# Linear ReLU attention on one core: first K and V issued inside the tile part, thirteen TensorE turns in one block, loads in runs of two, engines held to the last store

## Chip, core and metric

The kernel runs on one core of a Trainium2 chip. The metric is the device time of one execution in microseconds (us). For the kernel before, three runs gave a median of 124.86 us (124.73 to 124.92). A separate profiled execution took 124.66 us; its trace spans 123.4 us from the first to the last instruction of the program.

## What is computed

Q, K, V and the output are 8 x 12 x 512 x 64 in f32: 96 heads, 12.58 MB each. Cut to what matters:

```python
Q_feat = np.maximum(0, Q); K_feat = np.maximum(0, K)
KV = np.einsum('bhkd,bhkv->bhdv', K_feat, V)
K_sum = np.sum(K_feat, axis=2)
numerator = np.einsum('bhqd,bhdv->bhqv', Q_feat, KV)
denominator = np.einsum('bhqd,bhd->bhq', Q_feat, K_sum)
return numerator / (denominator[..., None] + 1e-10)
```

## The kernel before

**Tiling.** The 96 heads go in 12 octets of 8 heads. In an octet each of the 128 partitions holds 32 rows of one head, so Q, K, V and the output of an octet are each one transfer of 1.05 MB on the side of the DRAM. K and V of octet 0 come as f32 on the queues of SP and ACT (L94, L95) into two of the output buffers. All other loads are issued by POOL (L96, L109), which turns them into bf16 on the way, so they show as 512 KB.

**Buffers.** Loads go round a ring of six octets (`RING`, `slot`). Octet o is loaded when octet o-6 has been used: POOL waits on `PR1`, `VC` or `STG`. Results go round nine output buffers (`NOUT`). Each DMA has a semaphore of its own that counts 16 parts; `arrived` makes an engine wait for all 16 once.

**POOL's queue** is written out by hand: for each run of `RUNS` it issues K, V and Q of the run's octets in one DMA each, and ahead of a run the stores that are more than `RING + HEAD` octets behind. Before, each run has one octet and `HEAD` is 4, so store 0 stands ahead of the loads of octet 10, store 1 ahead of those of octet 11, and the rest behind. SP issues the last two stores, 10 and 11. The semaphore ahead of every store is `NRM1`.

**TensorE (PE)** runs `turn(i)` in a loop. In turn i, for octet i-1: 16 transposes of Q (L158; waits `STG`, and `DEN` after eight); 64 matmuls that accumulate K^T V with the row of K sums (L167; wait `VC`, `PR0`, `PR1`); 16 transposes that turn back the *previous* octet's numerators (L148, `back`; wait `OT`); 16 matmuls for the denominators (L176; wait `KVD`); 8 for the numerators (L184; wait `NRM0`, `NRM1`). After the twelve turns, `back` for octet 11 stands by itself behind the loop. An alignment to 256 instructions stands ahead of the loop.

**VectorE (DVE)**, in order for each octet o: wait `CK0`; `prep(o+1, 0)` (K features L237, needs K; V rows L241, needs V); `stage(o+1)` (copy of Q, L247, needs Q); `norm(o-1)` (two multiplies of 1.2 us, L259, write the output buffer; wait for `back`); `denominators(o)` (L265 to L273); `prep(o+1, 1)`. The engine works in order, so what waits for a load holds up everything behind it.

**ScalarE (ACT)**, for each octet: two ReLU evictions of Q^T (L214), four casts of K^T V (L219), V rows of the next octet (L208, needs V), two copies of the numerators (L228), which release `OT`.

**Head and tail.** The framework's part (`tc.close`, L15) ends with two barriers of all engines; then the kernel's own instructions begin, with 18 memsets and four operations on the identity on DVE. At the end SP waits for each store's semaphore in turn (L318) and clears the semaphores; the other engines run out of their programs when their work is done.

Of the kernel before, what the change touches and what calls it, by code (L numbers as in the profile page):

```python
# [5 lines left out]
def kernel(  # L6
# [4 lines left out]
    out: bass.AP,  # L11
):
    nc = tc.nc

    tc.close()  # L15
    tc.compile()

    B, H, S, D = Q.shape
    assert D == 64
    P = 128  # L20
    D1, D4 = D + 1, D + 4
    R = S * 4 // P
    RQ = 2 * R
    U = RQ // 2
    NO = B * H // 8
    assert NO * 8 == B * H and R == 16
    RING = 6
    NOUT = 9
    RUNS = (1,) * 11
    HEAD = 4  # L30

    fp32 = mybir.dt.float32
    bf16 = mybir.dt.bfloat16
    Act = mybir.ActivationFunctionType
    Alu = mybir.AluOpType
    PE, PL, VE, AC, SP = nc.tensor, nc.gpsimd, nc.vector, nc.scalar, nc.sync
# [25 lines left out]
    k8, v8 = o_sb[0], o_sb[1]  # L62
# [4 lines left out]
    vo = [sb(f"vo{i}", [P, R, 2, D4], bf16) for i in range(2)]  # L67
# [13 lines left out]
    ID, STG, PR0, PR1, DEN, NRM0, NRM1, DV = sems(  # L81
        "id", "stg", "pr0", "pr1", "den", "nrm0", "nrm1", "dv")
    VC, KVD, OT = sems("vc", "kvd", "ot")
    CQ0, CQ1, CK0, CK1, CB0, CB1, CD, CO0, CO1 = sems(
        "cq0", "cq1", "ck0", "ck1", "cb0", "cb1", "cd", "co0", "co1")
    landed = {}
    stored = sems(*[f"st{o}" for o in range(NO)])

    def land(name):
        landed[name], = sems(name)  # L90
        return landed[name]


    SP.dma_start(out=k8.rearrange("p r d -> p (r d)"), in_=Kr[0]).then_inc(land("k0"), 16)  # L94
    AC.dma_start(out=v8.rearrange("p r d -> p (r d)"), in_=Vr[0]).then_inc(land("v0"), 16)  # L95
    PL.dma_start(out=q_all[:, RING], in_=Qr[0], single_packet=True).then_inc(land("q0"), 16)  # L96
    run_of = {0: 0}

# [24 lines left out]
    o, done = 1, 0  # L123
# [6 lines left out]
    assert o == NO  # L130
    for i in range(done, NO - 2):
        store(PL, i)
    for i in range(NO - 2, NO):
        store(SP, i)

# [2 lines left out]
    def arrived(eng, c, o):  # L138
        s = landed[f"{c}{run_of[o]}"]
        if (eng.engine, s.num) not in seen:  # L140
            seen.add((eng.engine, s.num))
            eng.wait_ge(s, 16)

    def back(j):
        for v in range(8):
            t = PE.transpose(ps_o[j][:, P * v:P * v + P], ot[:, 8 * j + v].rearrange("p h c -> p (h c)"), ident32)  # L148
        t.then_inc((CB0, CB1)[j], 1)
# [35 lines left out]
                              start=True, stop=True, skip_group_check=True)  # L185
            t.then_inc((CO0, CO1)[j], 1)

    PE.wait_ge(ID, 4)
    with nc.Fori(1, NO + 1, engines=bass.OrderedEngineSet([PE.engine]), head_slot={PE.engine: 0}) as i:
        turn(i)  # L190
    PE.wait_ge(OT, NO + 1)
    back(0)
    back(1)


    def v_rows(o, g):
        rows = slice(R * g, R * g + R)
        return v_all[:, slot(o), rows] if o > 0 else v8[:, rows]
# [5 lines left out]
    def v_scalar(o):  # L204
        arrived(AC, "v", o)
        if o == 0:
            AC.wait_ge(ID, 4)
        AC.activation(vo[0][:, :, 1, 2:D + 2], v_rows(o, 0), Act.Copy, scale=mask_v[:, 1:2]).then_inc(VC, 1)  # L208

    v_scalar(0)  # L210
    for o in range(NO):
# [17 lines left out]
                        ps_o[j].rearrange("p (h u c) -> p u h c", h=4, u=U))  # L229
        t.then_inc(OT, 1)  # L230


    def prep(o, g):

        arrived(VE, "k", o)
        for s in range(2):
            VE.tensor_scalar(kf[g][:, :, s, :], k_rows(o, g), scalar1=0.0,  # L237
                             scalar2=mask_k[:, s:s + 1], op0=Alu.max, op1=Alu.mult)
        arrived(VE, "v", o)
        for t in range(1 + g):  # L240
            x = VE.tensor_scalar(vo[g][:, :, t, 2:D + 2], v_rows(o, g), scalar1=mask_v[:, t:t + 1],  # L241
                                 scalar2=None, op0=Alu.mult)
        x.then_inc((PR0, PR1)[g], 1)
# [5 lines left out]
    def norm(o):  # L249
        dst = o_sb[(o + 2) % NOUT]  # L250
        if o >= NOUT:
            VE.wait_ge(stored[o - NOUT], 16)
        VE.wait_ge(DV, 2 * o + 2 + DV0)
        if o == NOUT - 1:
            VE.wait_ge(VC, 1)
        for j in range(2):
            rs = slice(R * j, R * j + R)
            VE.wait_ge((CB0, CB1)[j], o + 2)
            VE.tensor_tensor(dst[:, rs], ps_o[j].rearrange("p (r d) -> p r d", d=D),  # L259
                             rec[o % 2][:, rs].unsqueeze(2).to_broadcast([P, R, D]),  # L260
                             op=Alu.mult).then_inc((NRM0, NRM1)[j], 1)
# [10 lines left out]
        VE.wait_ge(DV, 2 * o + 1 + DV0)  # L272
        VE.reciprocal(rec[o % 2], den).then_inc(DV, 1)  # L273

    for t in range(2):
        VE.memset(mask_v[:, t:t + 1], 0.0)
    VE.memset(kvd.rearrange("p h d -> p (h d)").bitcast(fp32), 0.0)
    VE.memset(ot.rearrange("p u h c -> p (u h c)"), 0.0).then_inc(OT, 1)
    ones = [vo[g][:, :, :, 1:D4 - 1][:, :, :, 0:D + 2:D1] for g in range(2)]
    VE.memset(ones[0], 0.0)  # L280
    VE.memset(ones[1], 0.0).then_inc(DV, 1)
    VE.wait_ge(DV, 1)
    for t in range(2):
        for half in range(2):
            b = 64 * half + 32 * t
            VE.memset(mask_v[b:b + 32, t:t + 1], 1.0)
            for g in range(2):
                VE.memset(ones[g][b:b + 32, :, t], 1.0)
    VE.wait_ge(ID, 2)
    VE.tensor_copy(ident32, ident).then_inc(ID, 1)  # L290
    VE.wait_ge(ID, 3)
    for c in range(2):
        VE.tensor_reduce(out=mask_h[:, :, c], in_=ident32.rearrange("p (h b) -> p h b", h=8),
                         op=Alu.add, axis=mybir.AxisListType.X)
    VE.tensor_reduce(out=mask_k, in_=ident32.rearrange("p (t s b) -> p s t b", t=4, s=2),
                     op=Alu.add, axis=mybir.AxisListType.XY).then_inc(ID, 1)
    DV0 = 1
    VE.wait_ge(ID, 4)
    for s in (DEN, NRM0, NRM1):
        VE.sem_inc(s, 1)  # L300
    prep(0, 0)
    prep(0, 1)
    stage(0)
    for o in range(NO):
        if o + 1 < NO:
            VE.wait_ge(CK0, o + 1)
            prep(o + 1, 0)
            stage(o + 1)
        if o > 0:
            norm(o - 1)  # L310
        denominators(o)
        if o + 1 < NO:
# [37 lines left out]
```

## Time and profile before

| what | value |
|---|---|
| median of three runs | 124.86 us |
| profiled execution | 124.66 us |
| its span | 123.4 us |
| PE, DVE, ACT, POOL busy | 71%, 72%, 64%, 22% of the span |
| HBM read and written | 37.75 MB and 12.58 MB: 408 GB/s over the span |
| DMA engines from 3 us to 120 us | busy 90% or more in each slice |
| first K and V issued | 1.40 us |
| last multiply on DVE (`norm(11)`, second half) | 115.41 to 116.64 us |
| last load (Q of octet 11) taken up by DVE | 98.52 us |

How to read it: the DMA line gives the busy share of the 16 DMA engines in 40 slices of 3.08 us. The line of GB/s counts what is written: a load that turns f32 to bf16 counts half, so 213 in the load stage and 425 in the store stage are the same 425 GB/s on the DRAM side. One transfer of an octet (1.05 MB there) takes 2.46 us at that rate, and there are 48 of them. In the timeline a row has the start, the busy time, the engine, the line, the operation and, in brackets, the idle time before it and what ended it. The page also lists two queues of kind "instruction": the engines' own fetches of their programs, which run on the same 16 DMA engines.

### The profile page before, as it was taken

The page shows a single profiled execution, that of the slowest core. Times are in us where ns is not written, and L with a number is a line of the kernel's source. Part 1 is how long each engine was busy: PE and PEld are TensorE (multiplying, and loading weights), DVE is VectorE, ACT ScalarE, POOL GpSimd, SP SyncE. Part 2 cuts the span into 40 slices and gives each one's busy share as a digit, 9 for nine tenths or more (in the row PEclk, how much of TensorE's full clock was granted, in tenths as well). Part 3 has the DMA queues.
Part 4 walks back from the last instruction along what each step waited for, and adds up shares of the span by engine and source line. Part 5 has one row for each costly group of instructions (what it writes and reads, how often), then busy time and mean ns, then how long its engine had stood idle before and what let it go on. Part 6 is the DMA issues. An engine that isn't in the chain of part 4 may idle for free.

```text
span 123.4 us, 3380 instructions
## 1 busy us (share of the span) xinstructions
PE 87.4 (71%) x1456; PEld 75.9 (62%) x1456; DVE 89.3 (72%) x178; ACT 79.4 (64%) x109; POOL 27.5 (22%) x50
## 2 busy tenths in 40 slices
PE   0000099998998979799897998979449939977400
PEld 0000099986886868688686877958429928947200
DVE  3737906599989899998989989897395497091600
ACT  0043063999988888898888889888539649542000
POOL 3999500050240804309101001010010001000000
PEclk9999999999999999999999999999985995996775
DMA  3999999999999999999999999999999999999994
GB/s 43 369 344 217 213 213 213 213 215 213 214 213 213 213 215 213 214 214 217 214 213 214 213 214 221 371 217 214 375 222 214 343 425 428 425 422 433 420 425 170
DMA packets 6918, 32.57 MB, mean 264 GB/s; under 512 B 768, under 2 KB 768, under 8 KB 5120
## 3 DMA queue, kind: packets, MB, share of 16 engines
q0 software_dynamic: 6336, 28.31, 92.2%
q1 hardware_dynamic: 432, 3.15, 6.6%
q10 hardware_dynamic: 144, 1.05, 2.2%
q8 instruction: 2, 0.03, 0.1%
q14 instruction: 4, 0.03, 0.1%
HBM read 37.75 MB, written 12.58 MB: 408 GB/s over the span
## 4 chain that ended last, share of the span: by engine, by line
DMA 34%; issue 27%; POOL 18%; PE 8%; DVE 5%; ACT 1%; POOLq 0%; DVEq 0%
DMA q_all<-in_Q_dram 34%; POOL k_all L109 6%; POOL q_all L109 5%; POOL v_all L109 5%; DVE o_sb L259 5%; PE ps_o L148 4%; PE ps_kv L167 2%; PE ps_q L158 1%; PE ps_o L184 1%; POOL out_dram L117 1%; ACT ot L228 1%; POOL q_all L96 1%; POOL ident L121 0%; POOL ident L119 0%; POOLq L107 0%
## 5 line engine op out<-in xcount | busy, mean ns | idle before, releaser
L259 DVE TENSOR_TENSOR o_sb<-ps_o,rec 128x1024 f32<-128x1024 f32 x24 | 28.3, 1219 | 7.0 <-PE ps_o L148 6.7
L228 ACT COPY ot<-ps_o 128x1024 f32<-128x1024 f32 x24 | 24.2, 1013 | 10.3 <-PE ps_o L184 9.2
L167 PE MATMUL ps_kv<-vo,kf 64*128 64x132 bf16 x768 | 28.6, 230 | 0.7
L148 PE MATMUL ps_o<-ident,ot 128*128 128x128 f32 x208 | 27.1, 286 | 1.1 <-ACT ot L228 1.1
L167 PEld LDWEIGHTS ps_kv<-vo,kf 64*128 64x128 bf16 x768 | 24.8, 100 | 3.8 <-DVE vo L241 2.3
L214 ACT ACTIVATE qt_sb<-ps_q 128x1024 bf16<-128x1024 bf16 x24 | 23.4, 1030 | 5.1 <-PE ps_q L158 5.1
L158 PE MATMUL ps_q<-ident,q_sb 128*128 128x128 bf16 x192 | 15.3, 243 | 15.4 <-DVE q_sb L247 15.4
L148 PEld LDWEIGHTS ps_o<-ident,ot 128*128 128x128 f32 x208 | 23.8, 146 | 2.7 <-ACT ot L228 1.4
L158 PEld LDWEIGHTS ps_q<-ident,q_sb 128*128 128x128 bf16 x192 | 13.2, 110 | 16.7 <-DVE q_sb L247 15.4
L219 ACT CAST kvd<-ps_kv 64x260 bf16<-64x260 f32 x48 | 18.0, 375 | 7.8 <-PE ps_kv L167 7.4
L184 PE MATMUL ps_o<-qt_sb,kvd 128*128 128x256 bf16 x96 | 15.0, 282 | 10.8 <-DVE o_sb L259 9.8
L237 DVE TENSOR_SCALAR kf<-k_all,mask_k 128x1024 bf16<-128x1024 bf16 x44 | 18.3, 459 | 5.6 <-PE ps_kv L167 5.4
L184 PEld LDWEIGHTS ps_o<-qt_sb,kvd 128*128 128x128 bf16 x96 | 7.7, 100 | 15.6 <-DVE o_sb L259 15.0
L241 DVE TENSOR_SCALAR vo<-v_all,mask_v 128x1024 bf16<-128x1024 bf16 x33 | 15.0, 483 | 0.9 <-DMA v_all<-in_V_dram 0.9
L109 POOL DMA_DIRECT2D k_all<-in_K_dram x11 | 8.4, 763 | 32.1 <-DVE vo L241 32.0
L117 POOL DMA_DIRECT2D out_dram<-o_sb x10 | 5.3, 533 | 40.7 <-DVE o_sb L259 40.7
L208 ACT ACTIVATE vo<-v_all,mask_v 128x1024 bf16<-128x1024 bf16 x11 | 12.7, 1155 | 0.3
L247 DVE COPY q_sb<-q_all 128x2048 bf16<-128x2048 bf16 x12 | 8.3, 694 | 5.7 <-DMA q_all<-in_Q_dram 5.7
L109 POOL DMA_DIRECT2D q_all<-in_Q_dram x11 | 8.9, 811 | 0.0
L109 POOL DMA_DIRECT2D v_all<-in_V_dram x11 | 7.6, 687 | 0.0
L176 PE MATMUL ps_q<-kvd,qt_sb 128*128 128x16 bf16 x192 | 6.9, 180 | 0.0
L176 PEld LDWEIGHTS ps_q<-kvd,qt_sb 128*128 128x128 bf16 x192 | 6.7, 96 | 0.2
(24 smaller groups left out, 27.8 us busy)
## 6 DMA issues: line engine op xcount, KB each, us to landing
out_dram<-o_sb POOLq DMA_DIRECT2D x10, 1024.0 KB, 39.8
q_all<-in_Q_dram POOLq DMA_DIRECT2D x12, 512.0 KB, 36.7
k_all<-in_K_dram POOLq DMA_DIRECT2D x11, 512.0 KB, 33.1
v_all<-in_V_dram POOLq DMA_DIRECT2D x11, 512.0 KB, 34.8
out_dram<-o_sb SPq DMA_DIRECT2D x2, 1024.0 KB, 8.4
o_sb<-in_K_dram SPq DMA_DIRECT2D x1, 1024.0 KB, 8.5
o_sb<-in_V_dram ACTq DMA_DIRECT2D x1, 1024.0 KB, 8.8
```

Source lines behind the costliest of these rows:

```text
L109: PL.dma_start(out=t[:, to:to + n], in_=X[o:o + n].rearrange("n p f -> p n f"), single_packet=True).then_inc(land(f"{c}{o}"), 16)
L148: t = PE.transpose(ps_o[j][:, P * v:P * v + P], ot[:, 8 * j + v].rearrange("p h c -> p (h c)"), ident32)
L158: t = PE.transpose(dst[:, u], q_sb[:, j * (U // 2) + u], ident)
L167: t = PE.matmul(ps_kv[:, half, 0:2 * (D + 2)].rearrange("p (t d) -> p t d", t=2), kf[g][rows, r].rearrange("p s d -> p (s d)"), vo[g][rows ...
L176: t = PE.matmul(ps_den[:, u], qt_sb[:, u], kvd[:, :, 0:2 * D1:2 * D1 - 1], start=True, stop=True, skip_group_check=True)
L184: t = PE.matmul(ps[:, h], kvd[:, 4 * j + h, 1:2 * D + 1], q[:, :, 4 * j + h, :], start=True, stop=True, skip_group_check=True)
L214: AC.activation(qt_sb[:, j * (U // 2):(j + 1) * (U // 2)], ps_q[j].bitcast(bf16).rearrange("p (u f) -> p u f", u=U // 2), Act.Relu)
L219: t = AC.copy(kvd[64 * c:64 * c + 64, s::2, c * D1:c * D1 + D1].rearrange("p (g t) d -> p g t d", t=2), ps_kv[64 * s:64 * s + 64, :, 0:2 * ...
L228: t = AC.copy(ot[:, :, 4 * j:4 * j + 4], ps_o[j].rearrange("p (h u c) -> p u h c", h=4, u=U))
L237: VE.tensor_scalar(kf[g][:, :, s, :], k_rows(o, g), scalar1=0.0, scalar2=mask_k[:, s:s + 1], op0=Alu.max, op1=Alu.mult)
L241: x = VE.tensor_scalar(vo[g][:, :, t, 2:D + 2], v_rows(o, g), scalar1=mask_v[:, t:t + 1], scalar2=None, op0=Alu.mult)
L259: VE.tensor_tensor(dst[:, rs], ps_o[j].rearrange("p (r d) -> p r d", d=D), rec[o % 2][:, rs].unsqueeze(2).to_broadcast([P, R, D]), op=Alu. ...
```

## The change

- K and V of octet 0 are issued inside the framework's part, in a critical section of SP and ACT, ahead of its closing barriers; PE's alignment moves ahead of that section.
- PE runs 13 turns instead of 12 and a separate `back`. The thirteenth works on old data up to `back`, which serves octet 11, and its last two parts are not used. Other engines raise `STG`, `PR0`, `PR1`, `VC`, `KVD` once more for it.
- DVE's setup shrinks from 18 memsets and four operations to two memsets and five operations; in `norm` the wait for `DV` goes, and `prep` gets one.
- `RUNS` becomes (1, 1, 2, 2, 2, 1, 1, 1): octets 3 and 4, 5 and 6, 7 and 8 are loaded in pairs, with one semaphore for each pair's K, V and Q. `HEAD` is 5, `NOUT` 11.
- At the end PE, ACT, DVE and POOL wait (`hold`) until all stores have landed, and then release SP. Nine stores share one semaphore, the last two another.

```diff
-    tc.close()
-    tc.compile()
...
-    NOUT = 9
-    RUNS = (1,) * 11
-    HEAD = 4
+    NOUT = 11
+    RUNS = (1, 1, 2, 2, 2, 1, 1, 1)
+    HEAD = 5
...
-    stored = sems(*[f"st{o}" for o in range(NO)])
+    ALL, LAST, FIN = sems("all", "last", "fin")
+    stored = [sems(f"st{o}")[0] if o + NOUT < NO else ALL if o < NO - 2 else LAST for o in range(NO)]
...
-    SP.dma_start(out=k8.rearrange("p r d -> p (r d)"), in_=Kr[0]).then_inc(land("k0"), 16)
-    AC.dma_start(out=v8.rearrange("p r d -> p (r d)"), in_=Vr[0]).then_inc(land("v0"), 16)
+    def hold(eng):
+        eng.wait_ge(ALL, 16 * (NOUT - 2))
+        eng.wait_ge(LAST, 32)
+        eng.sem_inc(FIN, 1)
+    PE.addr_align(256, offset=0, max_nops=0)
+    with tc.tile_critical(no_gpsimd_drain=True):
+        SP.dma_start(out=k8.rearrange("p r d -> p (r d)"), in_=Kr[0]).then_inc(land("k0"), 16)
+        AC.dma_start(out=v8.rearrange("p r d -> p (r d)"), in_=Vr[0]).then_inc(land("v0"), 16)
+    tc.close()
+    tc.compile()
...
-    PE.wait_ge(ID, 4)
-    with nc.Fori(1, NO + 1, engines=bass.OrderedEngineSet([PE.engine]), head_slot={PE.engine: 0}) as i:
+    with PE.Fori(1, NO + 2) as i:
         turn(i)
-    PE.wait_ge(OT, NO + 1)
-    back(0)
-    back(1)
+    hold(PE)
...
+    AC.wait_ge(KVD, NO)
+    AC.wait_ge(VC, NO)
+    AC.sem_inc(KVD, 1)
+    AC.sem_inc(VC, 1)
+    hold(AC)
...
+            if t and o:
+                VE.wait_ge(DV, 2 * o + DV0)
...
-        VE.wait_ge(DV, 2 * o + 2 + DV0)
+        if o == NO - 1:
+            VE.wait_ge(DV, 2 * o + 2 + DV0)
...
+    for s in (STG, PR0, PR1):
+        VE.wait_ge(s, NO)
+        VE.sem_inc(s, 1)
     norm(NO - 1)
-    for s in stored:
-        SP.wait_ge(s, 16)
+    hold(VE)
+    SP.wait_ge(CO1, NO + 1)
+    SP.wait_ge(FIN, 4)
```

More of the change, by code (lines that the diff above doesn't have):

```diff
@@ L66 @@
     kf = [sb(f"kf{i}", [P, R, 2, D], bf16) for i in range(2)]
-    vo = [sb(f"vo{i}", [P, R, 2, D4], bf16) for i in range(2)]
+    vo_all = sb("vo", [P, 2, R, 2, D4], bf16)
+    vo = [vo_all[:, i] for i in range(2)]
     kvd = sb("kvd", [P, 8, 2 * D1], bf16)
@@ L132 @@
         store(PL, i)
+    hold(PL)
     for i in range(NO - 2, NO):
@@ L206, in v_scalar @@
         if o == 0:
-            AC.wait_ge(ID, 4)
+            AC.wait_ge(ID, 5)
         AC.activation(vo[0][:, :, 1, 2:D + 2], v_rows(o, 0), Act.Copy, scale=mask_v[:, 1:2]).then_inc(VC, 1)
@@ L273, in denominators @@
         VE.reciprocal(rec[o % 2], den).then_inc(DV, 1)
-    for t in range(2):
-        VE.memset(mask_v[:, t:t + 1], 0.0)
-    VE.memset(kvd.rearrange("p h d -> p (h d)").bitcast(fp32), 0.0)
+    VE.memset(kvd.rearrange("p h d -> p (h d)").bitcast(fp32), 0.0).then_inc(DEN, 1)
     VE.memset(ot.rearrange("p u h c -> p (u h c)"), 0.0).then_inc(OT, 1)
[L279 to L288, printed above, removed]
     VE.wait_ge(ID, 2)
@@ L291 @@
     VE.wait_ge(ID, 3)
-    for c in range(2):
-        VE.tensor_reduce(out=mask_h[:, :, c], in_=ident32.rearrange("p (h b) -> p h b", h=8),
-                         op=Alu.add, axis=mybir.AxisListType.X)
+    VE.tensor_reduce(out=mask_v, in_=ident32.rearrange("p (a t b) -> p t a b", a=2, t=2),
+                     op=Alu.add, axis=mybir.AxisListType.XY).then_inc(ID, 1)
     VE.tensor_reduce(out=mask_k, in_=ident32.rearrange("p (t s b) -> p s t b", t=4, s=2),
-                     op=Alu.add, axis=mybir.AxisListType.XY).then_inc(ID, 1)
-    DV0 = 1
+                     op=Alu.add, axis=mybir.AxisListType.XY).then_inc(NRM0, 1)
+    VE.tensor_reduce(out=mask_h, in_=ident32.rearrange("p (h b) -> p h b", h=8).unsqueeze(2).to_broadcast([P, 8, 2, 16]),
+                     op=Alu.add, axis=mybir.AxisListType.X).then_inc(NRM1, 1)
     VE.wait_ge(ID, 4)
-    for s in (DEN, NRM0, NRM1):
-        VE.sem_inc(s, 1)
+    VE.tensor_copy(vo_all.rearrange("p g r t d -> p (g r) t d")[:, :, :, 1:D4 - 1][:, :, :, 0:D + 2:D1],
+                   mask_v.unsqueeze(1).unsqueeze(3).to_broadcast([P, 2 * R, 2, 2])).then_inc(ID, 1)
+    DV0 = 0
+    VE.wait_ge(ID, 5)
     prep(0, 0)
```

## The prediction

> **What bounds the kernel now.** I read the slices of the page first, then the DMA queues, the tail in small windows, and DVE's timeline. From the page:
>
> ```profile
> DMA  3999999999999999999999999999999999999994
> ...
> q8 instruction: 2, 0.03, 0.1%
> q14 instruction: 4, 0.03, 0.1%
> ```
>
> No engine bounds it: the transfers fill the span from the second slice to the last but one. 48 transfers of 2.46 us are 118.0 us of the 123.4. What can be won lies at the head, the tail, and in how evenly the 16 DMA engines finish. The last two rows are the engines' fetches of their own programs; they look like nothing. But the windows of the tail:
>
> ```profile
> 120.00:121.00 1.00, 0.00 (x0) 0.00 (x0) 0.00 (x0) 0.00 (x0) 0.00 (x0) 0.50 0.99 418
> 121.00:121.50 0.50, 0.00 (x0) 0.00 (x0) 0.00 (x0) 0.00 (x0) 0.00 (x0) 0.50 0.59 246
> 121.50:122.00 0.50, 0.00 (x0) 0.00 (x0) 0.00 (x0) 0.00 (x0) 0.00 (x0) 0.50 0.20 82
> 122.20:122.40 0.20, 0.00 (x0) 0.00 (x0) 0.00 (x0) 0.00 (x0) 0.00 (x0) 0.50 0.10 41
> ```
>
> The last two columns are DMA share and GB/s. The share falls to 0.2 at 121.5: for 1.2 us only a few DMA engines still work. The single records of the trace say which: the last store's 16 parts land at 121.55 to 121.93 (twelve), 122.68, 122.70, 123.04 and 123.14. One of the 16 is late all through: K of octet 1 has 15 parts by 13.74 and the last at 14.79, Q of octet 4 by 40.95 and 41.83. It becomes late between 11.2 and 13.4, where queue 8 has a 16,384-byte packet at 11.50 that takes 0.94 us. The other late engines appear after instruction packets at 97.46, 105.55 and 114.35. So a fetch makes one DMA engine late by 0.9 to 1.2 us, and every transfer ends with its latest engine.
>
> The second thing is how much room compute has. DVE's timeline:
>
> ```profile
> 34.46 0.69 DVE L247 COPY q_sb<-q_all 128x2048 bf16<-128x2048 bf16 x1 [0.19 <-DMA q_all<-in_Q_dram]
> 41.85 0.69 DVE L247 COPY q_sb<-q_all 128x2048 bf16<-128x2048 bf16 x1 [0.22 <-DMA q_all<-in_Q_dram]
> ...
> 71.35 0.69 DVE L247 COPY q_sb<-q_all 128x2048 bf16<-128x2048 bf16 x1 [0.43 <-DMA q_all<-in_Q_dram]
> 71.96 2.35 DVE L259 TENSOR_TENSOR o_sb<-ps_o,rec 128x1024 f32<-128x1024 f32 x2
> 79.28 2.35 DVE L259 TENSOR_TENSOR o_sb<-ps_o,rec 128x1024 f32<-128x1024 f32 x2
> 99.13 2.35 DVE L259 TENSOR_TENSOR o_sb<-ps_o,rec 128x1024 f32<-128x1024 f32 x2
> 107.76 2.36 DVE L259 TENSOR_TENSOR o_sb<-ps_o,rec 128x1024 f32<-128x1024 f32 x2 [3.62 <-PE ps_o L148]
> 110.94 0.35 DVE L273 RECIPROCAL rec<-den 128x32 f32<-128x32 f32 x1
> 115.41 1.23 DVE L259 TENSOR_TENSOR o_sb<-ps_o,rec 128x1024 f32<-128x1024 f32 x1 [0.38 <-PE ps_o L148]
> ```
>
> `norm` comes every 7.33 us (from 27.96 to 71.96 six times). DVE's pieces on that round, from norm to the end of `prep(., 1)`, are 5.0 us; half the K^T V matmuls (1.15) and half of `back` (1.0) close it at about 7.3: it is compute's own pace. Three loads take 7.37. So compute has no speed in hand: what it loses to a late load it does not win back. The last store is issued at 116.70, the transfers end at 121 to 123: some 2 us of room.
>
> TensorE's rows show the price of a pause: 16 transposes take 1.06 us in the steady rounds, 1.91 after 1.4 us of idling.
>
> ```profile
> 82.14 1.06 PE L158 MATMUL ps_q<-ident,q_sb 128*128 128x128 bf16 x16
> 102.06 1.91 PE L158 MATMUL ps_q<-ident,q_sb 128*128 128x128 bf16 x16
> ```
>
> **The change part by part.** I add against the profiled execution: 124.66, of which 123.36 is the span and 1.30 lies around it.
>
> *K and V earlier.* SP's waits:
>
> ```profile
> SPq L334 <- PEq L334: 0.7, 1, 0.7
> SPq L16 <- PEq L16: 0.5, 2, 0.3
> ```
>
> The first barrier (0.7) stays; the two of the closing (0.5) move behind the issue, which was at 1.40. New ahead of it are a branch and a semaphore that SP sends to itself and ACT. Gain at most 1.40 - 0.75 = 0.65, at least 0; I take 0.35, by the 0.5 less something. The Trainium skill, Advanced Engine Details and Errata, Control Flow Timing, gives about 51 ns for a branch; by that alone the gain would be 0.45. POOL's first load, issued at 1.93, moves behind SP's and ACT's issue (0.38 each) and the same two barriers, about 0.7 later, and all POOL's loads with it. K and V of octet 0 occupy the DMA engines until about 9, and Q of octet 0 isn't read before 14.67, so that is covered; uncovered it would cost the 0.7.
>
> *Shorter setup.* DVE's setup ends at 7.2 and then it waits 2.75 for K: costs and gains nothing.
>
> *Program fetches.* PE's alignment now stands as its fourth instruction, and 253 instructions follow to the end, less than a block of 256. So the fetch seen at 11.50, on entering the loop's block, moves to about 1 us, when no transfer runs; that at 114.35, on leaving it, goes. DVE fetches after about 64 of its instructions (32.75) and about 188 (97.46); its program falls from 211 to 187, so the second goes, if narrowly. The packet at 105.55 follows POOL's end (102.3), which `hold` puts off. What remains, at 32.75 and 49.67, leaves under 0.4 a few transfers later. The transfers then end at 121.93 - 0.35 = 121.6 instead of 123.14, and Q of octet 4 is there at 40.95 - 0.35 = 40.6 instead of 41.83. If the fetches stay: 0.9 more in both. The Trainium skill, Runtime: NRT & Kernel Launch, Instruction fetch mechanics, speaks against this gain: crossing a block is one DMA tail bump, mostly hidden. It counts the engine's stall; the trace shows the cost elsewhere, in the 0.94 us packet among the loads.
>
> *Runs of two.* The same bytes in fewer transfers: no gain in rate (a semaphore packet is 9 ns). But octet 3's Q now lands with octet 4's, at 40.6 instead of 34.46. DVE stands at `stage(3)`; behind it `norm(1)`, for which PE's numerators wait, so PE idles 6 us, and ACT's copies wait behind V. `norm(1)` starts at 40.6 + 0.61 (71.35 to 71.96) = 41.2. The next round begins cold: 8.6 by the round from 99.13 to 107.76; ends 7.33 and 9.3. Then eight rounds of 7.33 = 58.6. Octets 5 and 7 don't wait again (their Q at 55.4 and 70.1, DVE there at 56.5 and 71.1). `norm(10)`: 41.2 + 8.6 + 58.6 = 108.4, where before it was 107.76, late through stores 0 and 1 ahead of the last loads; `HEAD` 5 takes one of these (2.46) away. `NOUT` 11 takes waits away that were met anyway.
>
> *Thirteenth turn.* Before, `back` of octet 11 began 4.1 after norm(10), once ACT had copied, and cold (3.49). Now PE first transposes (1.0) and multiplies (2.27) old data, released by `STG`, which DVE raises after it has issued the reciprocal, 110.94 - 107.76 = 3.2 after norm(10); then half of `back` (1.0) and norm(11), 2.36. With 0.2 of hops: 10.1, where before it was 8.88. The store goes out at 118.5.
>
> *Last store.* K at the head took 1.0 from issue to its first packet (1.40, 2.41); eight packets of 0.306 per engine are 2.46: landed at 122.0. All other transfers are through at 121.6 - 2.46 = 119.1, so it runs alone.
>
> *End.* Before, 0.22 from landing to the end; `hold` adds one hop through four engines: 0.12, from 0 to 0.4. The new wait for `DV` in `prep` is met 1.3 us earlier by the reciprocal ahead of it: 0.
>
> Sum: 122.0 + 0.34 + 1.30 = 123.65. The median was 0.2 above the profiled execution: **123.8**.
>
> **Rivals.** *Transfers bound to the end.* If the cold round is 8.0 and the rounds 7.25, the store goes out before 118 and the end is 121.6 + 0.34 + 1.5 = 123.4. For it: 7.33 is a pace with 0.2 to 0.4 of waits for Q inside. Against: they fall inside the TensorE round.
>
> *The fetches are not what makes an engine late*, or move into the loads again. Then Q of octet 4 comes at 41.5, the store at 119.4, the end at 124.7. For it: a lag of 0.8 seen at 34.12 shrank again, that of 13.4 did not. That crossing is hidden, as Instruction fetch mechanics of the Trainium skill has it, would lead here too.
>
> *The thirteenth turn runs late and cold.* Each us of the last store beyond 118.5 counts in full, and from 119.6 on the kernel is slower than before. If the clock falls in PE's pauses there (0.5 and 0.3 us), transposes cost 0.85 more, the matmuls 1.0 (3.3 in the first octet), `back` 1.3 (3.49 for 1.97): store at 121.6, end 126.9. For it: the rows after 102 and 111.9. Against: in the steady rounds a pause of 0.52 never had this effect. A cold round of 9.3 adds 0.7.
>
> **How the numbers follow.** Forecast, 123.5 to 124.6: 0.52, faster. Transfers bound: 0.16, faster. Fetch lag stays: 0.14, of which 0.10 within 0.2% (0.25 us, about what a measurement here can tell from no change), 0.02 each side. Late thirteenth turn: 0.18, of which 0.16 slower, 0.02 the same. Faster 0.70, same 0.12, slower 0.18. The range is 122.9 (gain 0.65 at the head and no extra hop) to 125.8: it takes in two thirds of the last case.
>
> **What would show it.** First K issued near 1.05. No instruction packet between 3 and 30 us and none after 60; parts of a load landing within 0.5 of each other. `stage(3)` at 40.6, PE idle 6 us before it, then `norm` every 7.33. `norm(10)` at 108.4; 80 more K^T V and transposing matmuls on PE, before the last `back`; the last store issued near 118.5, DMA idle for half a microsecond before its data, end of span 122.3. Wrong would be: octet 3 not held up, or rounds of other than 7.3 us (the store's time moves by eight times that), or a late DMA engine still there at 15 us.

## The result and the profile after

The changed kernel takes 125.38 us (median of 12 runs, 125.10 to 126.74), the kernel before 124.85 beside it (12 runs, 124.65 to 125.15): ratio 1.0056, interval 1.0032 to 1.0080. It is slower by half a per cent where 123.8 was forecast. The profiled execution took 125.37, of which the span is 123.34, as good as before (123.36). So two things happened: the span kept almost nothing of the 1.06 us that it was to lose, and **2.03 us lie outside the span in place of 1.30**. Over the 12 runs, time less span is 2.07 in the median; for the kernel before it is 1.32.

The page of the profile shows that most packets of instructions went as forecast:

```profile
PEclk9999999999999559999999999999999999999997
DMA  3999999999999999999999999999999999999992
...
q8 instruction: 1, 0.02, 0.1%
q14 instruction: 2, 0.02, 0.0%
```

Queue 8 has one packet left, at 1.86, queue 14 two, at 35.62 and 55.52; none falls into the stores. The PEclk row (the clock granted to TensorE, in tenths) has a dip in the two slices from 40 to 46 us, at the end of TensorE's wait for octet 3 and behind it. DVE's timeline shows that wait and the rounds behind it:

```profile
40.78 0.69 DVE L265 COPY q_sb<-q_all 128x2048 bf16<-128x2048 bf16 x1 [4.44 <-DMA q_all<-in_Q_dram]
41.39 2.35 DVE L278 TENSOR_TENSOR o_sb<-ps_o,rec 128x1024 f32<-128x1024 f32 x2
...
49.64 2.36 DVE L278 TENSOR_TENSOR o_sb<-ps_o,rec 128x1024 f32<-128x1024 f32 x2
...
56.91 2.36 DVE L278 TENSOR_TENSOR o_sb<-ps_o,rec 128x1024 f32<-128x1024 f32 x2 [0.35 <-PE ps_o L161]
...
107.81 2.36 DVE L278 TENSOR_TENSOR o_sb<-ps_o,rec 128x1024 f32<-128x1024 f32 x2 [2.31 <-PE ps_o L161]
...
115.30 2.36 DVE L278 TENSOR_TENSOR o_sb<-ps_o,rec 128x1024 f32<-128x1024 f32 x2 [3.97 <-PE ps_o L161]
```

`stage(3)` at 40.78, norm(1) at 41.39, a cold round of 8.25, then seven of 7.26 or 7.27 and one of 7.34: forecast were 40.6, 41.2, 8.6 and 7.33. TensorE's timeline has the cold start (matmuls slowed behind a pause) and, 68 us later, the thirteenth turn:

```profile
42.66 2.17 PE L197 MATMUL ps_o<-qt_sb,kvd 128*128 128x256 bf16 x8 [6.38 <-DVE o_sb L278]
44.63 1.91 PE L171 MATMUL ps_q<-ident,q_sb 128*128 128x128 bf16 x16
...
111.07 1.07 PE L171 MATMUL ps_q<-ident,q_sb 128*128 128x128 bf16 x16 [0.24 <-DVEq L327]
112.07 2.07 PE L180 MATMUL ps_kv<-vo,kf 64*128 64x132 bf16 x64
114.07 1.97 PE L161 MATMUL ps_o<-ident,ot 128*128 128x128 f32 x16
```

The transposes take 1.91 behind 6.38 us of idling and 2.17 us of matmuls, and 1.07 in the thirteenth turn, which so runs warm. The last store is issued at 117.7 (forecast 118.5). Up to there the forecast holds. The tail does not (windows; the last two columns are DMA share and GB/s):

```profile
118.00:119.00 1.00, 0.33 (x4) 0.05 (x1) 0.00 (x0) 0.00 (x0) 0.00 (x0) 1.00 0.81 336
...
120.00:121.00 1.00, 0.00 (x0) 0.00 (x0) 0.00 (x0) 0.00 (x0) 0.00 (x0) 1.00 0.96 401
121.00:121.50 0.50, 0.00 (x0) 0.00 (x0) 0.00 (x0) 0.00 (x0) 0.00 (x0) 1.00 0.13 49
121.50:122.00 0.50, 0.00 (x0) 0.00 (x0) 0.00 (x0) 0.00 (x0) 0.00 (x0) 0.70 0.04 16
122.00:122.50 0.50, 0.00 (x0) 0.00 (x0) 0.00 (x0) 0.00 (x0) 0.00 (x0) 0.50 0.08 33
```

From 121.5 on a share of 0.04 to 0.08 is one of 16 engines. By the single records, 15 parts of the last store land between 121.31 and 121.68, and **the 16th at 123.11**. Before, four engines were late (122.68, 122.70, 123.04, 123.14). Now it is one, and the end is where it was.

By the landings it is not the engine that the packet at 1.86 made late. The trace doesn't number the engines, but the landings of the 16 parts can be followed from transfer to transfer, each against the middle of its 16. In the loads after that packet one engine is about 0.6 us behind (about 1.2 before), from the packet at 35.62 on a second one nearly as much. In the stores these two stay 0.5 to 0.6 behind, while a third one, at most 0.1 behind at 96.6 us, falls back: 0.44 at 99 us, 1.17 at 106, 1.51 at 111, 1.69 at the last store.

Between 96 and 118 us some of the stores' 8 KB packets take 320 to 400 ns in place of 309: 38 of them over 325, 1.7 us above 309 in all, mostly in rows one behind the other, as one engine works them off. That is about what the third engine loses. At the end it doesn't wait for work: from 117 us on no gap between its packets is over 0.03 us, its part of the store before lands at 120.67, and its last part 2.44 us later, the time of eight packets. The kernel before has such packets too (20, and 0.7 us, without the two of over 600 ns beside packets of instructions), and an engine that falls back with them from 0.15 at 99.6 us to 0.85 at 112; the prediction put all the lag of the tail to the instructions.

### The profile page after: what moved, and what is told of

Its sections match the earlier page's. It is cut to its first block, busy times and chain, and to the rows that moved or that the text cites. A ratio compares the mean times of both kernels' runs of the same rounds, so it can differ in the third digit from the quotient of the medians.

```text
span 123.3 us, 3566 instructions
## 1 busy us (share of the span) xinstructions
PE 88.8 (72%) x1560; PEld 76.5 (62%) x1560; DVE 87.9 (71%) x163; ACT 79.3 (64%) x109; POOL 22.4 (18%) x41
## 4 chain that ended last, share of the span: by engine, by line
DVE 39%; DMA 26%; PE 23%; POOL 5%; issue 2%; POOLq 0%; DVEq 0%
DMA q_all<-in_Q_dram 26%; DVE o_sb L278 21%; PE ps_kv L180 11%; PE ps_o L161 8%; DVE vo L259 5%; DVE kf L253 4%; DVE den L289 3%; DVE own L284 2%; DVE rec L292 2%; PE ps_q L171 2%; POOL k_all L120 1%; POOL v_all L120 1%; PE ps_o L197 1%; POOL q_all L120 1%; DVE q_sb L265 1%
## 5 line engine op out<-in xcount | busy, mean ns | idle before, releaser
L180 PE MATMUL ps_kv<-vo,kf 64*128 64x132 bf16 x832 | 29.4, 223 | 0.8
L197 PE MATMUL ps_o<-qt_sb,kvd 128*128 128x256 bf16 x104 | 16.6, 286 | 12.7 <-DVE o_sb L278 12.1
L161 PE MATMUL ps_o<-ident,ot 128*128 128x128 f32 x208 | 25.6, 276 | 0.0
L161 PEld LDWEIGHTS ps_o<-ident,ot 128*128 128x128 f32 x208 | 22.5, 141 | 1.4
L197 PEld LDWEIGHTS ps_o<-qt_sb,kvd 128*128 128x128 bf16 x104 | 8.5, 101 | 18.3 <-DVE o_sb L278 16.3
L120 POOL DMA_DIRECT2D k_all<-in_K_dram x8 | 5.4, 675 | 43.9 <-DVE vo L259 43.7
L189 PE MATMUL ps_q<-kvd,qt_sb 128*128 128x16 bf16 x208 | 7.5, 180 | 0.0
L189 PEld LDWEIGHTS ps_q<-kvd,qt_sb 128*128 128x128 bf16 x208 | 7.3, 96 | 0.2
L284 DVE SCALAR_TENSOR_TENSOR own<-ps_q,mask_h 128x256 f32<-128x256 f32 x12 | 5.0, 416 | 1.4 <-PE ps_q L189 1.4
L120 POOL DMA_DIRECT2D v_all<-in_V_dram x8 | 6.0, 745 | 0.0
```

The source lines that it names most:

```text
L120: PL.dma_start(out=t[:, to:to + n], in_=X[o:o + n].rearrange("n p f -> p n f"), single_packet=True).then_inc(land(f"{c}{o}"), 16)
L180: t = PE.matmul(ps_kv[:, half, 0:2 * (D + 2)].rearrange("p (t d) -> p t d", t=2), kf[g][rows, r].rearrange("p s d -> p (s d)"), vo[g][rows ...
L189: t = PE.matmul(ps_den[:, u], qt_sb[:, u], kvd[:, :, 0:2 * D1:2 * D1 - 1], start=True, stop=True, skip_group_check=True)
L197: t = PE.matmul(ps[:, h], kvd[:, 4 * j + h, 1:2 * D + 1], q[:, :, 4 * j + h, :], start=True, stop=True, skip_group_check=True)
```

## The experiments

The table has every run. "Outside" is time less span, run by run, in medians; ratios are to runs of the kernel before on the same chip, whose median was between 124.75 and 124.96.

| kernel | time | ratio [interval] | span | outside |
|---|---|---|---|---|
| before | 124.85 | 1 | 123.4 | 1.32 |
| changed | 125.38 | 1.0056 [1.0032, 1.0080] | 123.3 | 2.07 |
| e1, changed, no hold | 125.12 | 1.0043 [1.0020, 1.0066] | 123.4 | 1.71 |
| e2, before, with hold | 125.10 | 1.0031 [1.0015, 1.0048] | 123.35 | 1.73 |
| e3, changed, no pairs | 125.10 | 1.0027 [1.0008, 1.0047] | 123.0 | 2.03 |
| e4, changed, K and V late | 126.49 | 1.0161 [1.0130, 1.0191] | 124.15 | 2.34 |
| e5, changed, stores by SP | 125.74 | 1.0088 [1.0056, 1.0121] | 123.5 | 2.05 |
| e6, changed, loop entered as before | 125.54 | 1.0053 [1.0029, 1.0076] | 123.5 | 2.02 |
| e7, before, K and V early | 124.30 | 0.9961 [0.9939, 0.9983] | 122.95 | 1.32 |
| e8, no hold, no pairs, stores by SP | 124.46 | 0.9987 [0.9967, 1.0006] | 123.05 | 1.55 |
| e9, changed, no hold, old semaphores | 125.15 | 1.0013 [0.9996, 1.0030] | 123.45 | 1.71 |
| e10, before, new semaphores | 124.85 | 0.9996 [0.9977, 1.0016] | 123.5 | 1.37 |
| e11, e7 with thirteen turns | 124.24 | 0.9955 [0.9937, 0.9972] | 122.9 | 1.29 |
| e12, e9 without pairs | 124.42 | 0.9959 [0.9940, 0.9979] | 122.85 | 1.57 |
| e13, e1, longer DVE program | 125.16 | 1.0026 [1.0011, 1.0040] | 123.45 | 1.71 |
| e14, changed, longer DVE program | 125.53 | 1.0059 [1.0037, 1.0081] | 123.55 | 1.97 |
| e15, e12, longer DVE program | 124.33 | 0.9962 [0.9947, 0.9978] | 123.0 | 1.32 |
| e16, e7, short DVE program | 124.26 | 0.9956 [0.9937, 0.9974] | 122.95 | 1.31 |
| e17, e1, longer POOL program | 125.01 | 1.0019 [1.0005, 1.0033] | 123.35 | 1.68 |
| e18, changed, longer POOL program | 125.48 | 1.0051 [1.0034, 1.0069] | 123.45 | 2.02 |

The theory from this profile: hold costs about 0.7 us outside the span, and a late DMA engine sets the end of the span, so that nothing won ahead of it counts. Rivals: the time outside comes from issuing K and V in the tile part; the pairs of loads cost time at the end. Each kernel has one trace, of one execution, and its span can lie off the median of the table: by 0.4 in e3, 0.5 in e14, 0.6 in e8 and 0.9 in e5 (all longer).

**e1, hold taken out of the changed kernel.**

```diff
-    hold(PL)   # and PE, AC, VE
-    SP.wait_ge(FIN, 4)
+    SP.wait_ge(ALL, 16 * (NOUT - 2))
+    SP.wait_ge(LAST, 32)
```

> The changed kernel without hold: PE, ACT, DVE and POOL end when their own work is done, as in the kernel before; SP alone waits for the last stores. Theory (hold costs about 0.7 us that lies outside the span, since what each engine does after its last instruction now starts only when the last store has landed): time outside the span falls from about 2.0 back to about 1.3, span 123.1 to 123.3 or, if engines' ends fetch again and make another DMA engine late, up to 123.5; time 124.5 to 124.8, so 0.1 to 0.3% faster than before. Rival A (the time outside comes from the start, by K and V being issued inside the tile part): time outside stays at 2.0, time 125.3. Rival B (hold was what kept packets of instructions away from the tail): span rises by 0.5 or more.

Measured: outside 1.71, span 123.4, 125.12 us. Hold is worth 0.36 outside, half of what the theory wanted; 0.39 more than before is left. Rival A (2.0 outside) and rival B (0.5 more of span) fall.

**e2, hold alone put into the kernel before.**

```diff
+    hold(PL)   # and PE, AC, VE; stored[] counts in ALL and LAST
-    for s in stored:
-        SP.wait_ge(s, 16)
+    SP.wait_ge(FIN, 4)
```

> The kernel before with hold alone added to PE, ACT, DVE and POOL (and its three semaphores in place of the last nine). Theory: time outside the span rises from 1.3 to about 2.0; the span stays within 0.2 of 123.4, or falls by up to 0.3 where the packets of instructions at 105.55 and 114.35 followed engines' ends; time 125.2 to 125.6, so 0.3 to 0.6% slower than before. Rival A (time outside comes from the start): time 124.8, time outside 1.3.

Measured: outside 1.73, span as before. Hold costs 0.4 there, and its packets of instructions stayed where they were.

**e3, no pairs of loads.**

```diff
-    NOUT = 11
-    RUNS = (1, 1, 2, 2, 2, 1, 1, 1)
-    HEAD = 5
+    NOUT = 9
+    RUNS = (1,) * 11
+    HEAD = 4
```

> The changed kernel with the loads octet by octet, HEAD 4 and NOUT 9 as before; all else as changed. Theory (the transfers' one late DMA engine sets the end, and the compute had room): octet 3 is not held up, norm(10) 1 to 3 us earlier than 107.81 or held by stores, last store issued at 115.5 to 117.5, and the end of the span still 123.0 to 123.4; time as changed, 125.2 to 125.5. Rival (the wait for octet 3's Q and the cold round cost time at the end): span 122.0 to 122.5, time 124.2 to 124.7.

Measured: span 123.0 (122.6 to 123.5), between the two: the pairs cost some 0.3 here, where "the pairs" stands for `RUNS`, `HEAD` and `NOUT` together, which no run takes apart. In its trace, of an execution with a span of 123.4, norm(10) comes at 107.81 as with pairs, not the 1 to 3 us earlier that were expected. The last part is again late, 1.40 behind the middle, but another way: that engine was 1.40 behind at 92 us already, while loads still came in.

**e4, K and V issued behind the closing again.**

> The changed kernel with the issue of K and V of octet 0 moved back behind the closing of the tile part (the alignment stays ahead). Theory: first K issued at about 1.4 in place of 0.95, all transfers and the end 0.45 later, span 123.7, time outside unchanged at 2.0, time 125.8. Rival A (issuing inside the tile part adds 0.7 outside the span): time outside 1.3, time 125.0. Rival C (the 16 KB packet of instructions at 1.86 runs among the first packets only because K starts earlier; K later leaves it to itself): the late engine is late by less, and the span stays at 123.3 or falls.

```diff
-    with tc.tile_critical(no_gpsimd_drain=True):
-        SP.dma_start(... Kr[0]) ...; AC.dma_start(... Vr[0]) ...
     tc.close()
     tc.compile()
+    SP.dma_start(... Kr[0]) ...; AC.dma_start(... Vr[0]) ...
```

SP's waits in e4 (us in total, times, longest), and the issue in its timeline:

```profile
SPq L102 <- PEq L102: 0.9, 2, 0.6
```

```profile
1.82 0.38 SPq L103 DMA_DIRECT2D o_sb<-in_K_dram  x1
```

K goes out at 1.82, not at 1.4: the alignment makes TensorE branch at 0.83 for 0.31 us, it comes late to the closing's barrier, and everyone waits 0.9 there where it was 0.5. So behind the alignment, early issue is worth 0.87 at the issue. That the span is longer by nearly the same 0.85 is a coincidence, since it is not the transfers that end it here. Octet 4's Q is taken up at 42.14 in place of 40.78 and the cold round takes 9.08 in place of 8.25, so norm(10) comes at 109.98, 2.17 later, and the last store goes out at 119.9:

```profile
112.37 7.83 SPq L126 DMA_DIRECT2D out_dram<-o_sb  x2
```

Its 16 parts land between 123.50 and 123.90, none of them late. The DMA engines had run dry (share 0.20 between 119 and 120), so this end is compute's. Here 7.83 spans from the start of the first issue to the end of the second, which takes 0.33. The time outside did not fall, it rose to 2.34: it doesn't come from issuing K and V early.

**e5, the stores issued by SP.** The stretched packets had a candidate.

```diff
-    for i in range(done, NO - 2):
-        store(PL, i)
     hold(PL)
-    for i in range(NO - 2, NO):
+    SP.wait_ge(landed["v11"], 16)
+    for i in range(done, NO):
         store(SP, i)
```

> The changed kernel with the stores of octets 1 to 9 issued by SP (once V of octet 11 has landed) in place of POOL; all else as changed. In the trace of the changed kernel some packets of stores take 320 to 400 ns in place of 309 between 96 and 118 us, about 2.0 us in all, nearly all on one of the 16 DMA engines, and no load's packet does. Theory A (a DMA engine is slowed by what POOL's queue needs for its descriptors): the stretched packets go, the last part of a store follows the others by 0.6 as in the loads, and the transfers end about 1.0 earlier: span 122.2 to 122.5, time 124.2 to 124.6. Theory B (that engine writes DRAM more slowly, whoever issues): the stretched packets stay, the last store's last part is again 1.3 to 1.7 behind, span 123.0 to 123.6, time 125.2 to 125.6. Either: a gap of up to 0.5 us where SP's queue takes over from POOL's.

Between 96 and 108 us, 24 packets on SP's queue take over 325 ns, 1.06 us beyond 309 in all; on POOL's queue in the changed kernel it was 22 with 1.06. Theory A falls: the stretch goes with the stores, not with who issues them. The tail windows of e5:

```profile
121.00:121.50 0.50, 0.00 (x0) 0.00 (x0) 0.00 (x0) 0.00 (x0) 0.00 (x0) 0.50 1.20 508
...
122.00:122.50 0.50, 0.00 (x0) 0.00 (x0) 0.00 (x0) 0.00 (x0) 0.00 (x0) 0.50 0.04 16
...
123.00:124.00 1.00, 0.00 (x0) 0.00 (x0) 0.00 (x0) 0.00 (x0) 0.00 (x0) 0.50 0.04 16
```

One engine works on alone past 123, 2.1 us behind (this is the trace with a span of 124.4, the longest of e5's seven). The Trainium skill, DMA: Bandwidth & Descriptors, Latency and other measured facts, knows of two DMA engines, 7 and 15, that are usually slower and gives as a best guess the descriptor rings of GpSimd's queue, "SWDGE-specific". The stores here are stretched on SP's queue as they were on POOL's (24 packets and 22), so the two traces speak against that guess for the lag of the stores; they can't say whether the late engine is one of the two. About half of the 2.1 is older: six load packets at 88 us take 0.46 to 1.4 us, and two engines are 1.1 behind when the stores begin.

**e6, TensorE's loop entered as before, thirteen turns kept.**

```diff
-    PE.addr_align(256, offset=0, max_nops=0)
-    with PE.Fori(1, NO + 2) as i:
+    with nc.Fori(1, NO + 2, engines=bass.OrderedEngineSet([PE.engine]), head_slot={PE.engine: 0}) as i:
```

> The changed kernel with TensorE's loop entered as before (aligned at the loop, not as the program's start), still thirteen turns. Theory: the 16 KB packet of instructions is back at about 11.5, one DMA engine is 1.2 us behind in every load from octet 1's V on (0.65 as changed), yet the span stays at 123.2 to 123.6, since the stores' own late engine sets the end; and the time outside the span falls by about 0.4 from 2.05 to 1.65, if the alignment at the start is what adds the part of it that hold does not: time 124.9 to 125.2. Prediction's step (fetches set the end): span 123.9 to 124.4. Rival for the time outside (it comes from issuing K and V in the tile part, or from other programs' lengths): stays at 2.0, time 125.3 to 125.6.

The packet is back (at 7.44, not 11.5) and one engine is 1.3 behind in all loads, 0.65 more than in the changed kernel. The span grows by 0.2. By the landings that engine stays about 1.67 behind from 97 to 111 us, and another falls back from 0.2 to 1.63 in the same stores; the last two parts land at 122.81 and 123.25. So the prediction's step, that the fetches set the end, falls. That crossing a block is "mostly hidden", as the Trainium skill has it (Runtime: NRT & Kernel Launch, Instruction fetch mechanics), is near the truth for the time, 0.2 of 125, though not for the loads. The time outside stays at 2.02: the alignment at the start isn't its cause.

**e7, the kernel before with K and V early and nothing else.**

```diff
-    tc.close()
-    tc.compile()
...
+    with tc.tile_critical(no_gpsimd_drain=True):
         SP.dma_start(... Kr[0]) ...; AC.dma_start(... Vr[0]) ...
+    tc.close()
+    tc.compile()
```

> The kernel before with K and V of octet 0 issued inside the tile part, ahead of its closing; nothing else. Theory: first K issued at 0.95 in place of 1.40, all transfers 0.45 earlier, time outside unchanged at 1.3: span 122.9 to 123.1, time 124.2 to 124.4, 0.3 to 0.4% faster than before. Rival (issuing there is what adds 0.4 outside the span): time outside 1.7, time 124.6 to 124.8, as before.

e7's timeline, where before SP and ACT issued at 1.40:

```profile
0.91 0.39 ACTq L92 DMA_DIRECT2D o_sb<-in_V_dram  x1
0.95 0.38 SPq L91 DMA_DIRECT2D o_sb<-in_K_dram  x1
```

Span 122.95, outside 1.32, 124.30 us: the whole gain of the change is in this one part, 0.4%.

**e8, no hold, no pairs, the stores by SP** (e1, e3 and e5 together).

> The changed kernel without hold, without the loads of two octets (NOUT 9, HEAD 4 as before) and with the stores of octets 2 to 9 on SP. Theory A: no stretched store packets, no octet held up: last store issued at about 116, transfers through at 121.2 to 122.0, time outside 1.7: time 123.1 to 124.0, faster than the kernel before. Theory B: the late engine stays, span 122.6 to 123.2, time 124.3 to 124.9.

124.46, theory B: issuing the stores from SP's queue gains nothing.

**e9 and e10, the semaphores.** e9 is e1 with a semaphore for each store; e10 is the kernel before with ALL and LAST but no hold.

```diff
-    stored = [sems(f"st{o}")[0] if o + NOUT < NO else ALL if o < NO - 2 else LAST for o in range(NO)]
+    stored = sems(*[f"st{o}" for o in range(NO)])
```

> The changed kernel without hold and with a semaphore for each store again, all twelve of which SP waits for at the end, as before. Without hold alone, 1.71 us lay outside the span, 0.39 more than the 1.32 of the kernel before. Theory S (the three counting semaphores in place of nine add that 0.4): outside 1.32, span 123.4, time 124.7. Theory P (another program's length or shape adds it, TensorE's thirteen turns or the shorter VectorE program): outside 1.7, time 125.1.

> The kernel before with the counting semaphores ALL and LAST for the last nine stores in place of one for each, and no hold: SP alone waits for them. With hold as well it had 1.73 outside the span. Theory S: outside 1.73 here too, time 125.1, and hold itself costs nothing in the kernel before. Theory H (hold alone adds 0.4 there): outside 1.32, time 124.75 to 124.9.

e9 1.71, e10 1.37: the semaphores change nothing, and hold alone is the 0.4 of e2.

**e11, e7 with TensorE's thirteen turns**, entered as before, with the releases that they need on ACT and DVE.

```diff
-    with nc.Fori(1, NO + 1, engines=bass.OrderedEngineSet([PE.engine]), head_slot={PE.engine: 0}) as i:
+    with nc.Fori(1, NO + 2, engines=bass.OrderedEngineSet([PE.engine]), head_slot={PE.engine: 0}) as i:
         turn(i)
-    PE.wait_ge(OT, NO + 1)
-    back(0)
-    back(1)
```

> The kernel before with K and V early and TensorE's thirteen turns, the loop entered as before; no hold, no loads of two, the old setup and semaphores. Beside the kernel with K and V early alone (span 122.95, outside 1.32, time 124.30). Theory P: outside 1.7, if the thirteenth turn's program is what adds it; time 124.6 to 124.8. Otherwise outside 1.32. Span: norm(10) at about 107.3 as there, the last store issued about 10 after it in place of 8.9, at 117.2 instead of 116.2: still ahead of the other stores' end (118.8), so the span stays within 0.2 of 122.95; if it is issued after 118.8 it grows by the difference.

124.24, span 122.9, outside 1.29, the last store issued at 117.0 (116.3 in e7). The thirteenth turn is free here, where the store stands behind other stores.

**e12, e9 without the pairs.**

> The changed kernel without hold, without counting semaphores and without the loads of two octets (NOUT 9, HEAD 4): what is left are K and V early, the alignment at the start, thirteen turns and the shorter setup. Theory: span as without the pairs, 122.6 to 123.2, since a slow DMA engine sets the end of the stores; outside 1.32 by theory S (time 123.9 to 124.5, as fast as K and V early alone), 1.7 by theory P (time 124.3 to 124.9).

Beside e9 this is the price of the pairs: 0.73 us, 0.6 of it in the span. SP's last two stores in its timeline and one window, first of e9:

```profile
111.02 7.83 SPq L119 DMA_DIRECT2D out_dram<-o_sb  x2
```

```profile
118.00:119.00 1.00, 0.48 (x5) 0.31 (x4) 0.50 (x1) 0.00 (x0) 0.00 (x0) 1.00 0.32 131
```

Then of e12:

```profile
108.59 7.83 SPq L119 DMA_DIRECT2D out_dram<-o_sb  x2
```

```profile
118.00:119.00 1.00, 0.00 (x0) 0.00 (x0) 0.00 (x0) 0.00 (x0) 0.00 (x0) 1.00 0.95 401
```

So the last store is issued at 118.5 in e9 and at 116.1 in e12. In e9 most DMA engines run dry between 118 and 119; in e12 they don't. The changed kernel lies between (117.7, share 0.81). But the engine that ends e9's span is not one of those that run dry: its part of the store before lands at 120.89 and its last part at 123.30, 2.41 later, while the other 15 are through at 122.32. What fits the 0.6 is the stretch: store packets over 325 ns between 96 and 118 us cost 1.71 us in e9 and 1.15 in e12. That is one trace of each, and no run takes the stretch away by itself.

**e13 to e18, what else lies outside.** Hold explains 0.36 to 0.4 of the 0.75, the rest was open. As compiled, the changed kernel has 63 instructions on POOL and 187 on DVE, the kernel before 68 and 211; a packet of 8 KB on queue 14 at 125.06 in e3 and at 124.34 in e12, behind the span's end, suggested that a program which ends short of its next fetch ends more slowly. The traces of the changed kernel and of e1, with as much time outside, have no such packet.

e13 and e14: 30 small fills of a scratch tile on DVE ahead of its first wait for K, without and with hold. e15: 26 of them in e12.

```diff
+    for x in range(30):
+        VE.memset(pad[:, x:x + 1], 0.0)
     DV0 = 0
     VE.wait_ge(ID, 5)
```

> The changed kernel without hold, and VectorE's program made longer by 30 small fills of a scratch tile ahead of its first wait for K (186 to 216 instructions; some 1.0 to 1.8 us, beside the 2 us that it waits for K there). Theory D (a VectorE program that ends before its third block of instructions is fetched makes the ends of the programs slower): an 8 KB packet on queue 14 returns in the last third of the span, and 1.3 lie outside in place of 1.71; span as without hold, 123.3 to 123.6; time 124.7. Otherwise: outside 1.7, time 125.1.

> The changed kernel as it is, with hold, and the same 30 fills on VectorE (187 to 217 instructions). Theory D and hold adding up: outside 1.65 to 1.75 in place of 2.07 (as in the kernel before with hold, 1.73, with 212 instructions); span 123.3, time 125.0. If hold alone makes VectorE's length matter: 1.3. If the length is not it: 2.07, time 125.4.

> The changed kernel without hold, without counting semaphores, without the loads of two octets, and with 26 small fills on VectorE ahead of its first wait for K (191 to 217 instructions). Theory D: outside 1.32 in place of 1.57, span 122.85 as without the fills, or up to 0.4 more if the packet of instructions that comes back makes another DMA engine late: time 124.1 to 124.5. Otherwise time 124.4, as without the fills.

e13 stayed at 1.71, e14 came to 1.97, both against theory D; e15 fell from 1.57 to 1.32, for it, while its time is that of e12 (124.33 and 124.42).

e16: DVE's short setup and its fewer waits in e7.

> The kernel before with K and V early and the short setup of the changed kernel on VectorE (and its fewer waits in norm): 188 instructions of VectorE in place of 213. Nothing else. Theory D: outside rises from 1.32 to 1.55 to 1.75, with a span of 122.95 as before or, as the packet at 97 is gone, up to 0.2 less: time 124.5 to 124.7. Otherwise outside 1.32, time 124.1 to 124.3.

Outside 1.31 with 188 instructions: against theory D.

e17 and e18: 12 fills on POOL behind its last load, without and with hold.

```diff
     assert o == NO
+    for x in range(12):
+        PL.memset(pad[:, x:x + 1], 0.0)
```

> The changed kernel without hold, and POOL's program made longer by 12 small fills of a scratch tile behind its last load, where it waits for stores anyway (62 to 74 instructions). Theory P (a POOL program that ends just short of its 64th instruction, at which the next block is fetched, makes that fetch fall into the closing): a packet on queue 14 at about 65 to 100 us is new, and 1.3 lie outside in place of 1.71; span 123.3 to 123.6; time 124.75. Otherwise: outside 1.7, time 125.1.

> The changed kernel as it is, with hold, and the same 12 fills on POOL (63 to 75 instructions). Theory P and hold adding up: outside 1.65 to 1.75 in place of 2.07, as in the kernel before with hold (1.73); span 123.3; time 125.0. Otherwise: outside 2.0 to 2.1, time 125.4.

1.68 and 2.02: theory P falls as well. So neither length alone gives back the 0.35 to 0.4. Among the kernels of the changed shape without hold, outside is 1.55 to 1.71 where POOL's program, DVE's or both are short, and 1.32 in the one where both are long (e15, which has no pairs either); that either short end is enough would fit these, but not e16 (1.31 with DVE at 188), and was not tried in the changed kernel itself. Nor is the extra time fixed by the program: of e8's twelve runs four have 1.35 to 1.42 outside and eight 1.55 to 1.64, and of e15's twelve one has 1.64 and the others 1.27 to 1.37. **This part stays open.**

## Why the prediction was wrong

It said faster; the kernel is slower. That the measured time lies inside the stated range is luck: that part of the range was meant for a rival, the late and cold thirteenth turn, which did not happen. By its own steps:

- **K and V earlier: right, a little small.** 0.95 in place of 1.40, a gain of 0.45 where 0.35 was taken; e7 shows that it reaches the end in full. POOL's first load came 1.0 later rather than 0.7 (2.93, the same in e7, which has no alignment there), covered as said.
- **Shorter setup: right.** e16 and e7 differ by 0.04.
- **Program fetches: right in the loads, wrong at the end.** No packet is left in the tail, and Q of octet 4 is there at 40.77 (forecast 40.6). The one packet at the start runs at 1.86 to 3.20, not at 1, among K's first packets (1.96); it still makes an engine 0.65 late in the loads. **The step that failed is "The transfers then end at 121.93 - 0.35 = 121.6 instead of 123.14".** 15 of 16 engines do end by 121.68. The sixteenth ends at 123.11, late by the stores' own stretched packets. The reading under the step was that the late engines of the tail all follow from packets of instructions. One of the four before did not: it fell back to 0.85 by 112 us with the 20 stretched packets, which were there to be seen and were not priced; and the packet at 105.55 left an engine 0.3 late, not 0.9 to 1.2. In the changed kernel such packets cost 1.7 us instead of 0.7, which the prediction could not read from any row. The end is the latest of 16 engines, so causes of lag on different engines don't add: with the fetches of the tail gone, this engine stands where they stood, and a fetch put back among the loads (e6) costs only 0.2.
- **Runs of two: right**, within 0.2 at 41 and 0.6 at norm(10) (107.81, forecast 108.4). The cold round was forecast at 8.6; it took 8.25 here, 8.83 in e9 and 9.08 in e4. The prediction carried it to the last store but never said what the pairs cost by themselves: 0.3 (e3) to 0.6 (e12) of span.
- **Thirteenth turn: right.** 9.88 from norm(10) to the store's issue, forecast 10.1 (its terms add up to 10.0), warm; e11 shows that by itself it costs no time, though more stretched packets come with it (last section).
- **Last store:** at 117.7 it did not run alone, and 15 of its parts landed 3.6 to 4.0 later (forecast 3.5), the sixteenth 5.4 later.
- **End: the second step that failed is "+1.30", the time around the span held constant.** Inside the span `hold` is cheap as forecast: SP's wait for FIN ends 0.06 after the last landing. Outside it adds 0.36 (e1) and 0.41 (e2; e10 has the semaphores without hold, and 1.37). The cause that fits is that what each engine does behind its last instruction can no longer run beside the last stores; no row shows that part, so this is argued. A further 0.35 to 0.4 came with the rest of the change and is unexplained.

In sum: the span was missed by 1.0 (123.3 for 122.3), the time around it by 0.57 (2.07 for 1.30 + 0.2). Of the rivals, the lag that stays came nearest in kind (124.7), with the wrong cause; none had a cost outside the span.

The parts, each by its nearest pair of kernels: K and V early -0.57 (e7); the thirteenth turn and DVE's setup within 0.1 (e11, e16); the pairs with `HEAD` and `NOUT` +0.7 (e12 to e9) or +0.3 (e3 to changed); hold +0.26 to +0.35 (e1 to changed, before to e2). In the first price of the pairs 0.6 is span, and the rest time outside. **The best version is the kernel before with K and V early**, alone or with the thirteen turns: 124.30 and 124.24, ratios 0.9961 and 0.9955. e16 (with the short setup), e12 (all of the change less hold, counting semaphores and pairs) and e15 (e12 with the longer DVE program) are not told apart from these.

## What to carry to other kernels

Where transfers bound a kernel, follow all 16 parts of a transfer through the kernel, not only the last one: ask which DMA engine is next when the latest is cured, and when it fell back. Time around the span is not a constant: an edit that changes how or when engines end has to be judged by the whole time, since the profile may show nothing of it. And a change of many parts is priced part by part: here one part won 0.57 us, and hold and the pairs, neither needed by it, lost at least as much.

## What the hardware showed that was not expected

- In the stage of pure stores, some 8 KB packets take 320 to 400 ns in place of 309, and one DMA engine falls back with them, in the changed kernel from at most 0.1 to 1.69 us. Which queue issues makes no difference (e5). Of the changed kernel's some 4,000 load packets behind the first 14 us 2 take over 325 ns, both just behind the packet of instructions at 35.62. Other traces have more: 218 in e3, and in e5 and several others a few load packets of 0.4 to 1.4 us between 74 and 97 us.
- The 20 traces fall into three groups by what their store packets over 325 ns cost between 96 and 118 us (packets over 600 ns, beside packets of instructions, left out). With twelve turns and no pairs it is 0.67 to 0.74 us (before, e2, e7, e10, e16), with thirteen turns and no pairs 1.14 to 1.34 (e3, e8, e11, e12, e15), with pairs, all of thirteen turns, 1.71 to 1.83 (changed, e1, e4, e5, e6, e9, e13, e14, e17, e18). So the thirteenth turn (e7 to e11) and the pairs (e12 to e9) each go with some 0.5 us more. Why is open.
- With hold, single runs took 0.6 to 1.2 us longer outside the span than the others (126.74 and 126.10 in the changed kernel, with 3.24 and 3.00; two runs of e4; one of e5). The other kernels with hold (e2, e3, e6, e14, e18) had no such run, and in the kernels without hold none came above 1.77.
- A branch to an aligned block as TensorE's first step takes 0.31 us and holds back a barrier of all engines by 0.42 (e4, 1.82 for 1.40). Where SP and ACT issue ahead of that barrier, as in the changed kernel, it is hidden: SP waits 0.5 at its two barriers as before.
